# RMS-norm factors of a two-layer decoder trunk: from logarithm, exponential and a Newton step to GpSimd's power operation

## The chip, the core and the metric

One core of one Trainium2 chip runs the whole kernel. The metric is the device time of one execution in microseconds (us), as a median of several runs. The core's engines are PE (TensorE: matmuls, with the weight loads PEld), DVE (VectorE), ACT (ScalarE), POOL (GpSimd) and SP (SyncE, which here only issues DMAs). Each engine works through its own queue in order.

## The reference, cut to what matters

Two layers act on 512 tokens of width 1024 in float32. Layer 0 mixes with an mLSTM (4 heads), layer 1 with stick-breaking attention (16 heads); each layer then cross-attends into 256 memory tokens and applies a SwiGLU FFN of width 2816. Every sub-layer is normalised before and after:

```python
def rms_norm(x, gain):
    y = x * lax.rsqrt(jnp.mean(x * x, axis=-1, keepdims=True) + RMS_EPS)
    return y * gain
...
for layer in range(2):
    y = mixer(rms_norm(x, g[0]));                        x = x + rms_norm(y, g[1])
    y = memory_cross_attention(rms_norm(x, g[2]), mem_n); x = x + rms_norm(y, g[3])
    y = swiglu_ffn(rms_norm(x, g[4]));                   x = x + rms_norm(y, g[5])
```

The memory tokens are normalised once (`mem_n`), and the mLSTM normalises each head's output over its 256 columns. So each norm needs one factor per token, the reciprocal root of a mean square plus 1e-6; with 128 tokens on the partitions that is a 128x1 tile (128x4 for the four mLSTM heads).

## The kernel before

**Work.** All weights stream from HBM. Most products run in float32r on a high and a low part of each operand (`split`, L525: ACT or DVE copies the high part, DVE subtracts for the low part), three matmuls per product (`mm3`). Large projections use a seven-product block scheme (`seven`, L638), in which some weight blocks are summed by accumulating DMAs on POOL's queue (`gather`, L415): such a DMA waits until DVE and ACT have read the old block, and PE needs its sum.

**Order.** The program does not fix the order by hand. `Plan.op` (L148) records each operation with a cost in ns; `Plan.lay_out` (L195) then plays list scheduling over PE, ACT, DVE, POOL and SP, with costs, hand-over latencies (L138) and a limited number of buffers (L36 to L42: 44 big ones, 8 PSUM banks), and the instructions are emitted in the order of the planned starts. An operation on POOL is planned at 110 ns plus 3.4 ns per element (L446), a DMA issue on POOL at 1040 ns (L412). ACT's functions live in tables: Exp and Ln share one, Tanh, Sigmoid and Silu have others (L357); a change of table is planned at 1300 ns (L137), and the load of the Exp/Ln table is emitted at L339. Since the whole order comes out of the planned costs, any change of an operation moves others too.

**Norms.** `sumsq` (L733) squares a tile on ACT and accumulates the sum per token. `rstd` (L738) makes the factor: DVE scales the sum (L743), ACT takes the logarithm (L745) and the exponential of minus one half of it (L746), and DVE does a Newton step in two instructions (L748 and L751), three for the 128x4 tile. Where a row of 1024 is summed in two halves, `rest` (L754) turns the first half's sum into two biases by two DVE instructions. Factors are used in four places:

- `arrive` (L1546): 4 tiles of the input x, at the start; the first tile in halves.
- `heads` (L985): 4 factors of 128x4, for the mLSTM heads. The four PSUM banks of a token tile stay occupied until DVE has multiplied them by the factor (L1005). In the same stage the gates use Sigmoid.
- `boundary` (L816): after each mixer, cross-attention and FFN, 4 token tiles. Each tile has a factor for the post-norm (L841), whose product DVE adds to the residual (L846), and, but for the last boundary, a factor for the next pre-norm (L856), after which the tile is scaled (L859) and PE transposes it (L860). That is 24 and 20 factors. POOL also issues the loads of the gains (L763) and the spills of x (L855).
- `memory` (L1293): 2 tiles, by `rsqrt` (L719), a root by bit shift and three Newton steps, all on DVE.

At the last boundary `out` is stored by SP (L847) after L846.

Of the kernel before, what the change touches and what calls it, by code (L numbers as in the profile page):

```python
# [11 lines left out]
I32 = mybir.dt.int32  # L12
# [4 lines left out]
P = 128  # L17
# [355 lines left out]
class Trunk:  # L373
# [79 lines left out]
    def ts(self, out, a, s1, s2, op0, op1=None):  # L453
        def fn(nc):
            kw = {} if op1 is None else {"op1": op1}
            nc.vector.tensor_scalar(out=ap(out), in0=ap(a), scalar1=ap(s1), scalar2=ap(s2), op0=op0, **kw)  # L456

        self._dve(out, [a], fn, fast=True, scalars=(s1, s2))
# [260 lines left out]
    def rsqrt(self, y, v, n=1):  # L719

        vh, bits, u = self.small(n), self.small(n, I32), self.small(n)
        self.ts(vh, v, -0.5, None, ALU.mult)
        self.ts(bits, v.bitcast(I32), 1, None, ALU.logical_shift_right)
        self.ts(y.bitcast(I32), bits, -1.0, float(0x5F3759DF), ALU.mult, ALU.add)
        for _ in range(3):
            if n == 1:
                self.ts(u, y, y, vh, ALU.mult, ALU.mult)
            else:
                self.tt(u, y, y, ALU.mult)
                self.tt(u, u, vh, ALU.mult)  # L730
            self.stt(y, u, 1.5, y, ALU.add, ALU.mult)

    def sumsq(self, src, acc):  # L733

        junk = self.half(src.free, dt=BF16)
        self.act(junk, src, AF.Square, accum=acc)

    def rstd(self, ss, size, part=None):  # L738

        n = ss.free  # L740
        y, vh, u = self.small(n), self.small(n), self.small(n)
        b, bh = part if part else (self.eps, -0.5 * EPS)
        self.ts(vh, ss, -0.5 / size, bh, ALU.mult, ALU.add)  # L743
        self.act(y, ss, AF.Ln, scale=1.0 / size, bias=b)
        self.act(y, y, AF.Exp, scale=-0.5)  # L745
        if n == 1:  # L746
            self.ts(u, y, y, vh, ALU.mult, ALU.mult)
        else:  # L748
            self.tt(u, y, y, ALU.mult)
            self.tt(u, u, vh, ALU.mult)  # L750
        self.stt(y, u, 1.5, y, ALU.add, ALU.mult)  # L751
# [891 lines left out]
```

## Time and profile before

| | |
|---|---|
| time, median of 3 runs | 1495.97 us (1494.13 to 1496.73) |
| the profiled execution's own time | 1499.86 us |
| its span, first to last instruction | 1498.2 us |
| mean granted TensorE clock | 0.996 of 2.4 GHz |
| instructions | 26046 |
| bytes moved by DMA | 190.46 MB, 127 GB/s over the span |

The profiled execution is one run of its own; its time stands 3.9 us above the median. In the rows, an engine's busy time is the time in which an instruction of its own runs; "idle before" is what the engine waited, and the name behind the arrow is what ended that wait by the trace (for several awaited things, the one that came last). Line numbers are those of helpers where a helper records every operation: L505 is a matmul, L519 a transpose, L451 a two-input DVE operation, L456 DVE's tensor by scalars, L463 DVE's three-operand form, L429 an ACT function, L436 an ACT copy, L413 a DMA issue and L418 an accumulating DMA. Names are kinds of buffers: big, half, sm (the small tiles of the norms), ps (PSUM).

### The profile page before, as it was taken

The page shows a single profiled execution, that of the slowest core. Times are in us where ns is not written, and L with a number is a line of the kernel's source. Part 1 is how long each engine was busy: PE and PEld are TensorE (multiplying, and loading weights), DVE is VectorE, ACT ScalarE, POOL GpSimd, SP SyncE. Part 2 cuts the span into 40 slices and gives each one's busy share as a digit, 9 for nine tenths or more (in the row PEclk, how much of TensorE's full clock was granted, in tenths as well). Part 3 has the DMA queues.
Part 4 walks back from the last instruction along what each step waited for, and adds up shares of the span by engine and source line. Part 5 has one row for each costly group of instructions (what it writes and reads, how often), then busy time and mean ns, then how long its engine had stood idle before and what let it go on. Part 6 is the DMA issues. An engine that isn't in the chain of part 4 may idle for free. (4 is left out here: it accounts for less than half of the span.)

```text
span 1498.2 us, 26046 instructions
## 1 busy us (share of the span) xinstructions
PE 1470.4 (98%) x10346; PEld 1372.4 (92%) x10346; DVE 1214.7 (81%) x1920; ACT 863.6 (58%) x1533; POOL 142.6 (10%) x179
## 2 busy tenths in 40 slices
PE   6999899999999999999999999999999999999998
PEld 5999889998999999998889889888988999999996
DVE  7978879797887876888858998879787969768985
ACT  6668746474754454635548897756456635444632
POOL 2100100100111110110100000000000111110110
PEclk9999999999999999999999999999999999999999
DMA  7545747342654665565511215336514573854651
GB/s 240 113 85 115 223 129 237 71 128 85 203 107 100 132 150 129 118 145 187 166 32 29 71 45 182 113 119 175 143 57 140 116 167 58 205 119 86 141 170 56
DMA packets 166810, 190.46 MB, mean 127 GB/s; under 512 B 6944, under 2 KB 140576, under 8 KB 166688
## 3 DMA queue, kind: packets, MB, share of 16 engines
q1 hardware_dynamic: 119632, 121.16, 25.4%
q0 software_dynamic: 47056, 67.64, 23.0%
q8 instruction: 81, 1.33, 0.4%
q14 instruction: 41, 0.34, 0.1%
HBM read 176.72 MB, written 10.49 MB: 125 GB/s over the span
## 5 line engine op out<-in xcount | busy, mean ns | idle before, releaser
L505 PE MATMUL ps<-big,big 128*128 128x256 f32 (+2 forms) x9712 | 1407.3, 305 | 7.0 <-ACT big L436 3.5
L505 PEld LDWEIGHTS ps<-big,big 128*128 128x128 f32 x9712 | 1294.1, 189 | 93.5 <-ACT big L436 3.9
L451 DVE TENSOR_TENSOR big<-big,big 128x1024 fp32r<-128x1024 f32 (+1 forms) x516 | 607.2, 1210 | 48.9 <-ACT big L436 30.0
L436 ACT CAST big<-big 128x1024 fp32r<-128x1024 f32 (+1 forms) x385 | 391.2, 1044 | 139.9 <-DMA big<-in_ffn_w_gate_up_dram 42.1
L429 ACT ACTIVATE half<-ps 128x512 f32<-128x512 f32 (+4 forms) x185 | 92.5, 527 | 108.0 <-PE ps L505 99.7
L436 ACT COPY half<-ps 128x512 f32<-128x512 f32 (+2 forms) x105 | 61.4, 585 | 137.6 <-PE ps L505 124.9
L451 DVE TENSOR_TENSOR big<-ps,big 128x512 fp32r<-128x512 f32 (+3 forms) x188 | 109.6, 603 | 32.5 <-ACT big L436 20.3
L436 ACT CAST big<-ps 128x512 fp32r<-128x512 f32 (+2 forms) x164 | 80.2, 516 | 91.8 <-PE ps L505 55.2
L451 DVE TENSOR_TENSOR big<-half,big 128x512 fp32r<-128x512 f32 (+3 forms) x150 | 82.7, 575 | 9.3 <-ACT big L429 7.6
L429 ACT ACTIVATE half<-big 128x512 bf16<-128x512 f32 (+1 forms) x63 | 41.9, 665 | 73.1 <-DVE big L451 47.0
L418 POOL DMA_DIRECT2D big<-in_ffn_w_gate_up_dram x40 | 50.8, 1271 | 330.6 <-DVE big L451 171.1
L463 DVE SCALAR_TENSOR_TENSOR half<-ps,half 128x512 f32<-128x512 f32 (+3 forms) x74 | 47.2, 644 | 42.0 <-ACT half L436 22.3
L436 ACT CAST big<-half 128x512 fp32r<-128x512 f32 (+3 forms) x109 | 51.9, 529 | 23.1 <-DVE half L451 14.6
L519 PE MATMUL ps<-const,big 128*128 128x128 f32 (+1 forms) x314 | 44.2, 280 | 13.0 <-DVE big L463 9.9
L451 DVE TENSOR_TENSOR half<-ps,half 128x512 f32<-128x512 f32 (+2 forms) x78 | 46.9, 630 | 11.7 <-PE ps L505 8.1
L519 PEld LDWEIGHTS ps<-const,big 128*128 128x128 f32 (+1 forms) x314 | 37.9, 146 | 18.7 <-issue 10.3
L429 ACT ACTIVATE half<-half 128x512 f32<-128x512 f32 (+2 forms) x74 | 40.4, 588 | 21.1 <-DVE half L451 21.0
L451 DVE TENSOR_TENSOR big<-ps,gain 128x512 f32<-128x512 f32 x32 | 22.0, 686 | 33.4 <-ACT half L429 32.9
L429 ACT ACTIVATE big<-ps 64x512 fp32r<-64x512 f32 (+2 forms) x66 | 38.9, 590 | 11.9 <-PE ps L505 8.1
L505 PE MATMUL ps<-big,const 128*128 128x256 f32 (+3 forms) x224 | 40.5, 320 | 0.0
L505 PEld LDWEIGHTS ps<-big,const 128*128 128x128 f32 x224 | 35.6, 188 | 3.7
L463 DVE SCALAR_TENSOR_TENSOR big<-big,sm,gain 128x512 f32<-128x512 f32 (+1 forms) x47 | 36.3, 805 | 2.6 <-DMA gain<-in_norm_gains_dram 2.0
(85 smaller groups left out, 590.2 us busy)
## 6 DMA issues: line engine op xcount, KB each, us to landing
big<-in_ffn_w_gate_up_dram SPq DMA_DIRECT2D x68, 512.0 KB, 5.7
big<-in_ffn_w_gate_up_dram POOLq DMA_DIRECT2D x40, 512.0 KB, 6.0
big<-in_ffn_w_down_dram SPq DMA_DIRECT2D x36, 512.0 KB, 5.8
big<-in_xa_w_kv_dram SPq DMA_DIRECT2D x32, 512.0 KB, 5.3
big<-in_sb_w_qkv_dram SPq DMA_DIRECT2D x24, 512.0 KB, 3.9
big<-in_ml_w_in_dram SPq DMA_DIRECT2D x19, 512.0 KB, 5.5
dr<-big POOLq DMA_DIRECT2D x16, 512.0 KB, 4.9
big<-in_xa_w_o_dram SPq DMA_DIRECT2D x16, 512.0 KB, 6.2
```

What stands on the lines that cost most here:

```text
L418: "POOL", 1040, lambda nc: nc.gpsimd.dma_start(ap(out), ap(in_), accum_op=ALU.add), [in_, out], [out], load=ns
L429: nc.scalar.activation(ap(out), ap(in_), func, scale=ap(scale), **kw)
L436: "ACT", 0.833 * n + (60 if psum else 95), lambda nc: nc.scalar.copy(ap(out), ap(in_)), [in_], [out],
L451: self._dve(out, [a, b], lambda nc: getattr(nc, q).tensor_tensor(out=ap(out), in0=ap(a), in1=ap(b), op=op), eng)
L463: lambda nc: nc.vector.scalar_tensor_tensor(out=ap(out), in0=ap(a), scalar=ap(s), in1=ap(b), op0=op0, op1=op1),
L505: nc.tensor.matmul(ap(out), lhsT=ap(a), rhs=ap(b), start=start, stop=stop, **kw)
L519: nc.tensor.transpose(ap(out), ap(in_), ap(ident))
```

## The change

`sumsq` scales its input by one over the root of the size before it squares, so that the accumulated sum is the mean square. `rstd` becomes two POOL instructions: add epsilon (or the first half's prepared mean square), then raise to the power of a constant tile of -0.5. `rest` becomes one POOL addition. `rsqrt` goes, and the memory tokens use `rstd` too. The planner, its costs and all hand-written orders stay as they are; the schedule is laid out anew from the changed operations.

```diff
-    def ts(self, out, a, s1, s2, op0, op1=None):
+    def ts(self, out, a, s1, s2, op0, op1=None, eng="DVE"):
...
-    def sumsq(self, src, acc):
+    def sumsq(self, src, acc, size):
...
-        self.act(junk, src, AF.Square, accum=acc)
+        self.act(junk, src, AF.Square, scale=size**-0.5, accum=acc)
...
-    def rstd(self, ss, size, part=None):
-        n = ss.free
-        y, vh, u = self.small(n), self.small(n), self.small(n)
-        b, bh = part if part else (self.eps, -0.5 * EPS)
-        self.ts(vh, ss, -0.5 / size, bh, ALU.mult, ALU.add)
-        self.act(y, ss, AF.Ln, scale=1.0 / size, bias=b)
-        self.act(y, y, AF.Exp, scale=-0.5)
-        if n == 1:
-            self.ts(u, y, y, vh, ALU.mult, ALU.mult)
-        else:
-            self.tt(u, y, y, ALU.mult)
-            self.tt(u, u, vh, ALU.mult)
-        self.stt(y, u, 1.5, y, ALU.add, ALU.mult)
+    def rstd(self, ms, rest=None):
+        y = self.small(ms.free)
+        if rest is None:
+            self.ts(y, ms, EPS, None, ALU.add, eng="POOL")
+        else:
+            self.tt(y, ms, rest, ALU.add, "POOL")
+        self.tt(y, y, self.mhalf[:, 0 : ms.free], ALU.pow, "POOL")
         return y
-    def rest(self, ss):
-        b = self.small(2)
-        for i, m in ((0, 1.0), (1, -0.5)):
-            self.ts(b[:, i : i + 1], ss, m / D, m * EPS, ALU.mult, ALU.add)
-        return b[:, 0:1], b[:, 1:2]
+    def rest(self, ms):
+        b = self.small(1)
+        self.ts(b, ms, EPS, None, ALU.add, eng="POOL")
+        return b
...
-        self.eps = self.const(P, 1)
-        self.memset(self.eps, EPS)
+        self.mhalf = self.const(P, 4)
+        self.memset(self.mhalf, -0.5)
...
-            self.prenorm(m, m, g, steps=True)
+            self.prenorm(m, m, g)
```

The calls in `arrive`, `heads` and `boundary` change with these signatures alone.

## Rows read from the trace of the kernel before

**Rows 1.** The page, busy time, share of the span and instructions of each engine

```profile
PE 1470.4 (98%) x10346; PEld 1372.4 (92%) x10346; DVE 1214.7 (81%) x1920; ACT 863.6 (58%) x1533; POOL 142.6 (10%) x179
```

**Rows 2.** Stretches: length, busy us of PE, PEld, DVE, ACT, POOL; clock, DMA, GB/s

```profile
0.00:30.00 30.00, 18.40 (x77) 15.10 (x78) 19.85 (x39) 20.13 (x40) 9.59 (x37) 1.00 0.77 263
...
125.00:200.00 75.00, 70.02 (x498) 66.01 (x497) 60.37 (x174) 48.74 (x108) 9.94 (x15) 0.95 0.56 164
...
670.00:700.00 30.00, 27.39 (x206) 25.80 (x206) 25.06 (x30) 14.51 (x18) 1.87 (x4) 1.00 0.70 229
...
1485.00:1498.20 13.20, 5.83 (x26) 4.35 (x24) 6.53 (x14) 2.44 (x8) 0.00 (x0) 0.81 0.21 79
```

**Rows 3.** Timeline, head stage: start us, us, instruction, idle before

```profile
134.08 0.16 DVE L456 TENSOR_SCALAR sm<-sm 128x4 f32<-128x4 f32 x1
134.48 1.28 ACT L339 ACT_TABLE_LOAD   x1
...
136.36 1.27 POOL L418 DMA_DIRECT2D big<-in_ml_w_in_dram  x1 [18.07 <-DVE big L451]
...
140.73 0.46 DVE L463 SCALAR_TENSOR_TENSOR big<-ps,sm,big 128x256 f32<-128x256 f32 x1
...
141.24 5.01 PE L505 MATMUL ps<-big,big 128*128 128x256 f32 x40 [1.15 <-DVE big L463]
```

**Rows 4.** Timeline, the late gather after the head stage

```profile
153.90 1.28 POOL L418 DMA_DIRECT2D big<-in_ml_w_in_dram  x1 [1.29 <-DVE sm L456]
...
163.84 1.04 ACT L436 CAST big<-big 128x1024 fp32r<-128x1024 f32 x1 [3.27 <-DMA big<-in_ml_w_in_dram]
```

**Rows 5.** Busy time after the late gather, columns as in group 2

```profile
164.00:174.00 10.00, 8.18 (x44) 7.99 (x45) 6.77 (x14) 6.84 (x15) 0.53 (x1) 0.66 1.04 410
```

**Rows 6.** Waits of PE over the span: total us, times, longest us

```profile
PE ps L519 <- DVE big L451: 1.4, 1, 1.4
```

**Rows 7.** Timeline, the tail of the kernel

```profile
1492.12 0.19 ACT L429 ACTIVATION_READ_ACCUMULATOR half<-big 128x1 f32 x1
...
1492.47 0.68 DVE L451 TENSOR_TENSOR big<-big,gain 128x512 f32<-128x512 f32 x1
...
1493.57 1.41 DVE L463 SCALAR_TENSOR_TENSOR big<-big,sm,big 128x512 f32<-128x512 f32 x2
```

**Rows 8.** Waits of PE weight loads from 1100 to 1180 us

```profile
PEld ps L519 <- DVE big L463: 0.4, 1, 0.4
```

**Rows 9.** Groups of ACT instructions by shape: busy us, mean ns, idle before

```profile
L429 ACT ACTIVATE sm<-sm,sm 128x1 f32<-128x1 f32 x45 | 13.1, 294 | 2.0 <-DVE sm L456 0.7
...
L429 ACT ACT_TABLE_LOAD x8 | 10.3, 1283 | 0.1
L339 ACT ACT_TABLE_LOAD x8 | 10.3, 1283 | 0.1
L429 ACT ACTIVATE sm<-sm 128x1 f32<-128x1 f32 x48 | 9.7, 204 | 1.3
```

**Rows 10.** Groups of DVE instructions by shape

```profile
L451 DVE TENSOR_TENSOR big<-big,big 128x1024 fp32r<-128x1024 f32 x419 | 500.5, 1218 | 41.6 <-ACT big L436 29.3 <-PE ps L505 9.3 <-issue 1.6
...
L456 DVE TENSOR_SCALAR sm<-sm,sm 128x1 f32<-128x1 f32 x99 | 23.7, 242 | 16.5 <-ACT half L429 8.8 <-ACT sm L429 6.1
...
L456 DVE TENSOR_SCALAR sm<-sm 128x1 f32<-128x1 f32 x130 | 15.2, 147 | 11.7 <-ACT half L429 9.4
```

**Rows 11.** Groups of POOL instructions by shape

```profile
L487 POOL TENSOR_SCALAR_AFFINE_SELECT half<-half 128x128 f32<-128x128 f32 x2 | 0.6, 305 | 0.0
...
L482 POOL MEMSET const<- 128x1 f32 x1 | 0.1, 100 | 0.3 <-POOLq L1630 0.3
```

**Rows 12.** Timeline, the first 10 us

```profile
5.20 1.83 POOL L487 TENSOR_SCALAR_AFFINE_SELECT half<-half 128x512 f32<-128x512 f32 x3
...
6.10 0.94 DVE L463 SCALAR_TENSOR_TENSOR sm<-sm,sm 128x1 f32<-128x1 f32 x1
...
9.03 0.75 DVE L463 SCALAR_TENSOR_TENSOR big<-big,sm,gain 128x512 f32<-128x512 f32 x1 [1.98 <-DMA gain<-in_norm_gains_dram]
```

More of the change, by code (lines that the diff above doesn't have):

```diff
@@ L451, in tt @@
         self._dve(out, [a, b], lambda nc: getattr(nc, q).tensor_tensor(out=ap(out), in0=ap(a), in1=ap(b), op=op), eng)
-    def ts(self, out, a, s1, s2, op0, op1=None):
+    def ts(self, out, a, s1, s2, op0, op1=None, eng="DVE"):
+        q = {"DVE": "vector", "POOL": "gpsimd"}[eng]
         def fn(nc):
             kw = {} if op1 is None else {"op1": op1}
-            nc.vector.tensor_scalar(out=ap(out), in0=ap(a), scalar1=ap(s1), scalar2=ap(s2), op0=op0, **kw)
-        self._dve(out, [a], fn, fast=True, scalars=(s1, s2))
+            getattr(nc, q).tensor_scalar(out=ap(out), in0=ap(a), scalar1=ap(s1), scalar2=ap(s2), op0=op0, **kw)
+        self._dve(out, [a], fn, eng, fast=True, scalars=(s1, s2))
     def stt(self, out, a, s, b, op0, op1):
@@ L763, in gain, with prenorm @@
         return g
-    def prenorm(self, out, x, g, steps=False):
+    def prenorm(self, out, x, g):
         ss = self.small(1)
-        self.sumsq(x, ss)
-        if steps:
-            v, r = self.small(1), self.small(1)
-            self.ts(v, ss, 1.0 / D, EPS, ALU.mult, ALU.add)
-            self.rsqrt(r, v)
-        else:
-            r = self.rstd(ss, D)
-        self.stt(out, x, r, g, ALU.mult, ALU.mult)
+        self.sumsq(x, ss, D)
+        self.stt(out, x, self.rstd(ss), g, ALU.mult, ALU.mult)
     def acts(self, n=S):
@@ L835, in evac @@
             x = ps if not ys else y
-            self.sumsq(x, s)
+            self.sumsq(x, s, D)
             self.tt(y, x, g_post[:, sl], ALU.mult)
@@ L840, in evac @@
                 return
-            r = self.rstd(s, D, part[t])
+            r = self.rstd(s, part[t])
             x, y, ss2 = xs[t], yg[t], self.small(2)
@@ L848, in evac @@
                 else:
-                    self.sumsq(x[:, c], ss2[:, hf : hf + 1])
+                    self.sumsq(x[:, c], ss2[:, hf : hf + 1], D)
                     if hf == 0:
@@ L855, in evac @@
                 self.dma("POOL", spill[t], x)
-            r = self.rstd(ss2[:, 1:2], D, part[t])
+            r = self.rstd(ss2[:, 1:2], part[t])
             for hf in range(2):
@@ L994, in heads @@
                 self.tt(dh, ps[:, 256:257], dh, ALU.max)
-                self.sumsq(ps[:, 0:256], ss[:, hh : hh + 1])
+                self.sumsq(ps[:, 0:256], ss[:, hh : hh + 1], MLV)
                 nums.append(ps)
@@ L1000, in heads @@
             self.tt(vv, vv, rinv, ALU.mult)
-            y = self.rstd(vv, MLV)
+            y = self.rstd(vv)
             self.tt(y, y, rinv, ALU.mult)
@@ L1553, in arrive @@
         for i, c in enumerate(halves):
-            k.sumsq(xin[t][:, c], ss[:, i : i + 1])
-        r = k.rstd(ss[:, 1:2], D, k.rest(ss[:, 0:1]))
+            k.sumsq(xin[t][:, c], ss[:, i : i + 1], D)
+        r = k.rstd(ss[:, 1:2], k.rest(ss[:, 0:1]))
         for i, c in enumerate(halves):
```

11 lines of the change are left out of this document (removed).

## The prediction

> **What bounds the kernel.** I read the page first: PE is busy 1470.4 us of 1498.2, DVE 81%, ACT 58%, POOL 10% [rows 1]. PE's matmuls are the same before and after, so only PE's idle time and PE at a low clock can change: 27.8 us are idle in all. The second view cuts the span into stretches [rows 2]: 11.6 us of the idle time lie in the first 30 us, 5.0 between 125 and 200 us, 2.6 between 670 and 700, and 7.4 at the end; the other 1.2 us are strewn. The reader should see that DVE and ACT, which the change relieves, are not where the time is: what they save counts only where PE waits for them.
>
> Such a place is the mLSTM head stage. In its timeline [rows 3] the scaled squares of the first head tile are ready at 134.24 (134.08 + 0.16), but ACT must load the Ln/Exp table, goes back to Sigmoid, loads again, and the tile's first product starts at 140.73, 6.5 us later. The product frees a PSUM bank, and PE, idle for 1.15 us, starts at 141.24, 0.05 us after its end at 141.19. Then follows a stall whose owner is a transfer: an accumulating DMA is issued on POOL at 153.90, and ACT's copy of its block starts at 163.84 after waiting 3.27 us for it [rows 4]. With the 1.15 us and a wait of 1.41 us for DVE at 181 [rows 6] taken from the stretch's 4.98, this stall is 2.42 us. It also costs clock: in the 10 us after 164 the granted clock is 0.66 in the mean, thus at the lower level of 1.2 GHz for some 7 us, and 44 matmuls take 8.18 busy us [rows 5], where 40 took 5.01 at 141 [rows 3]. At that rate 44 take 5.5 us, so the clock costs 2.7 us. The stall was PE's idle time just before.
>
> The tail is read as a chain [rows 7]: the last accumulation ends at 1492.31 (1492.12 + 0.19), the last scaled products start at 1493.57: 1.26 us from sum to factor. Last I looked for norms that PE only just escapes: before the second FFN one transpose's weight load waited 0.4 us for DVE's scaled tile [rows 8].
>
> **The change, part by part.** *Off ACT.* 52 factors lose Ln and Exp, 0.294 and 0.204 us each by the rows for most of them [rows 9]: about 26 us. There are 17 table loads: the first, eight to Ln/Exp and eight to others, at 1.283 us [rows 9]. In the timeline I count which serve a norm alone: four in the head stage with the four that lead back, and the one before the last boundary; two more only move on to the next Exp. Nine go, 11.5 us. *Off DVE.* The first scaling and the Newton step (93 of the 99 instructions with two small operands, 22.5 us) and the two of `rest` for 45 sums with seven like them (97 of 130, 11.3 us) [rows 10], with some 12 us in smaller groups: 46 us of 1214.7. All this is hidden behind PE, except in the places above, so by itself it is worth nothing.
>
> *Onto POOL.* 54 factors of two instructions and 45 of `rest` make 153, on an engine that is busy 142.6 us [rows 1]. No arithmetic of one element stands in the trace on POOL. The nearest below is a memset of 128x1, 0.10 us; the nearest that reads SBUF is a select of 128x128, 0.305 us [rows 11]; the longest POOL instruction in these rows is a DMA issue, 1.27 us [rows 3]. I take 0.305 for the addition and for the power, 0.10 as the lower end of both, and 1.27 as the upper end of the power alone. Three hand-overs (ACT to POOL, POOL to itself, POOL to DVE) I take at the 0.05 us seen from DVE to PE. From sum to factor that is 0.15 + 0.61 = 0.76 us, between 0.35 and 1.73, against 1.26 now. At the tail this gives -0.5 us (-0.9 to +0.5). DVE's product with the gain, at 1492.47 [rows 7], now waits behind the scaling that goes; it will run before, so POOL finds DVE idle there.
>
> *The head stage.* The factor needs about 0.8 us and one small DVE product. POOL's queue is in order, and an accumulating DMA stands in it, waiting, until 136.36, and takes until 137.63 [rows 3]. Even behind that the factor is there by about 138.6, 2 us ahead of 140.73. So the 1.15 us go. But PE then comes to the late block 1.15 us sooner, so that stall shrinks only by as much as the block comes sooner. What hangs on norms there is ACT's and DVE's work in front of the DMA's issue: the ACT loads and functions named above are half of ACT's time from 134 to 154. What does not is the DMA itself: 9.9 us from issue to use, with the DMA engines at a share of 1.04 [rows 4, 5]. Of the 2.42 + 2.7 = 5.1 us I take one half, 2.6; the ends are 0 and 5.1. The wait at 181 stands in a stretch in which DVE works without a break, partly on the two memory factors by bit shift, 20 small instructions; I take 0.3 of its 1.41.
>
> *The start.* The first factor is ready at 7.04 and waits for the gain's DMA until 9.03 [rows 12]. With POOL busy on selects until 7.03 it may come 0.76 us after them, at 7.8: still covered. I take 0. If that cover went, 0.8 us would show.
>
> *Waits added.* A norm that waits at the head of POOL's queue holds back what is behind it: accumulating DMAs, gain loads, spills, and so weights for PE. In the FFNs, where most accumulating DMAs are, no norm runs; at the boundaries PE has matmuls to cover it. I take 0, and leave a loss to the second rival.
>
> Sum: -1.15 - 2.6 - 0.3 - 0.5 = -4.55 us. On the profiled execution's 1499.86 that gives 1495.3; the median of the runs is 3.9 us lower, so I forecast 1495.97 - 4.55 = **1491.4 us**. Its own range is 1487 to 1493: all of 5.1 and 0.9 at one end, a gain of 3 at the other. About 0.2%, 3.0 us, is what a measurement of this kernel can tell from no change.
>
> **The rivals.** *The stall moves.* If the late block is as late in absolute time as before, PE waits 1.15 us longer for it, and the whole head stage gives nothing; the sum is then -0.5 - 0.3, and the time 1495.2 (1493 to 1499, since the whole order is laid out anew and other waits of 1 to 3 us, such as the 2.6 us before 700, can come or go). For it speaks the DMA share of 1.04, against it that the DMA's issue itself waits on DVE and ACT.
>
> *POOL and DVE block each other.* In the first 10 us a DVE instruction on three 128x1 operands took 0.94 us, against a mean of 0.24 for others as small; it ended at 7.04, just as three POOL selects ended at 7.03 [rows 10, 12]. So a small DVE instruction was held until POOL was done, and the reverse must be feared: DVE's commonest instruction takes 1.218 us and stands there 419 times [rows 10]. If each POOL instruction waits half of one, 0.61 us, a factor takes 0.76 + 1.22 = 1.98 us, 0.72 more than now. Of the 40 factors of the five boundaries that are followed by transposes I take one in four as uncovered, since one weight load of a transpose already waits [rows 8]: 10 x 0.72 = 7.2 us, and 1503.2 us. It decides from the point where the factor takes longer than 1.26 plus what PE still has to do. Against it: PE idles nowhere at these boundaries now, and the factor's present way also waits for DVE's long instructions. The Trainium skill, page "SBUF — State Buffer", section "Who interferes with whom", states this as a rule: a DVE instruction with two SBUF inputs and a GpSimd one that reads SBUF exclude each other, and the later one waits for the whole of the first. By that rule this change is slower, and the 0.94 us agree with it; no row shows the reverse case, POOL held by DVE. A slow power alone, at its upper 1.27 us, works in the same place: 0.15 + 0.305 + 1.27 = 1.73 us are 0.47 more than now, 4.7 us on 10 factors.
>
> **How the numbers follow.** Forecast 0.50, moved stall 0.27, blocked POOL 0.23. So faster by over 0.2% 0.50, within 0.27, slower 0.23. The range runs from 1487 (the forecast with its best ends) to 1501, which takes in the moved stall and the milder part of the blocked POOL, and leaves out under 2 in 10.
>
> **What would show it.** Right: eight table loads; no Sigmoid load between two head tiles; no PE wait for DVE's product near 141; the late block's copy before 163 and a granted clock above 0.66 behind it; POOL powers near 0.3 us; sum to factor under 1.26 us at the tail. Wrong: powers over 1 us, POOL's norms starting as long DVE instructions end, waits of transposes on DVE's scaled tile at the boundaries, or accumulating DMAs issued later than now because a norm stands in front of them.

## The result, and the profile after

The changed kernel takes **1503.53 us** (median; 1501.89 to 1506.04), against 1495.74 us for the kernel before on the same chip: a ratio of 1.0053, 95% interval 1.0041 to 1.0065, so 7.8 us slower. The forecast was 1491.4 us, faster, with a range of 1487 to 1501. Of all executions below, one of the kernel with raised boundary prices and multiplications fell in a slower state (1788.08 us, granted clock 0.754 in the mean); ratios leave it out.

The page after, busy time, share of the span and instructions of each engine; then the stretches of [rows 2], with the same columns, and the 10 us of [rows 5]:

```profile
span 1501.8 us, 25849 instructions
...
PE 1471.7 (98%) x10346; PEld 1371.4 (91%) x10346; DVE 1178.0 (78%) x1649; ACT 830.1 (55%) x1421; POOL 219.0 (15%) x332
```

```profile
0.00:30.00 30.00, 19.09 (x87) 15.79 (x88) 18.16 (x23) 19.55 (x35) 15.77 (x47) 1.00 0.80 266
125.00:200.00 75.00, 71.49 (x507) 66.44 (x506) 58.21 (x139) 41.46 (x101) 23.54 (x34) 0.98 0.65 196
670.00:700.00 30.00, 30.00 (x216) 28.00 (x216) 27.03 (x32) 14.68 (x18) 1.45 (x3) 1.00 0.68 227
...
164.00:174.00 10.00, 9.20 (x79) 8.96 (x78) 9.24 (x17) 8.56 (x16) 2.42 (x3) 1.00 0.96 371
```

Against [rows 1], ACT is relieved by 33.5 us (37.5 reckoned) and DVE by 36.7 (46 reckoned), and POOL is 76.4 us busier. In the first two stretches PE idles 0.7 and 1.5 us less than in [rows 2], and behind the late block the clock is 1.00, against 0.66 [rows 5]. So up to there the head stage, which the forecast watched, is better. The 2.6 us of the third stretch are gone too, but a second profile of the kernel before lacks them as well. What is new is the list of transposes that wait for the tile they transpose. At the boundaries the kernel before has none of 0.15 us or more. This is the timeline of PE after, the seven of them:

```profile
236.50 0.66 PE L521 MATMUL ps<-const,big 128*128 128x128 f32 x4 [0.79 <-DVE big L465]
...
383.62 1.23 PE L521 MATMUL ps<-const,big 128*128 128x128 f32 x8 [0.75 <-DVE big L465]
...
707.81 0.63 PE L521 MATMUL ps<-const,big 128*128 128x128 f32 x4 [0.45 <-DVE big L465]
...
717.00 0.66 PE L521 MATMUL ps<-const,big 128*128 128x128 f32 x4 [0.47 <-DVE big L465]
...
731.58 0.63 PE L521 MATMUL ps<-const,big 128*128 128x128 f32 x4 [0.28 <-DVE big L465]
...
1014.48 0.66 PE L521 MATMUL ps<-const,big 128*128 128x128 f32 x4 [1.08 <-DVE big L465]
...
1150.65 1.23 PE L521 MATMUL ps<-const,big 128*128 128x128 f32 x8 [0.48 <-DVE big L465]
```

Together 4.3 us, spread over all five boundaries. In front of each stands a factor made on POOL. The groups of POOL (out<-in, shape, count, busy us, mean ns) give what one costs: the power, the additions of eps, and the additions of a prepared rest.

```profile
L451 POOL TENSOR_TENSOR sm<-sm,const 128x1 f32<-128x1 f32 x50 | 31.6, 632 | 3.4
L458 POOL TENSOR_SCALAR sm<-sm 128x1 f32<-128x1 f32 x50 | 21.0, 421 | 242.6 <-ACT half L429 241.2
...
L451 POOL TENSOR_TENSOR sm<-sm,sm 128x1 f32<-128x1 f32 x45 | 12.4, 276 | 105.7 <-ACT half L429 104.6
```

A power takes 0.57 us in the median (0.55 at least), an addition 0.19 to 0.22 where nothing holds it (spans on POOL are rough, but a product of DVE that waits for a free power also starts 0.60 us after the power did, 194.21 after 193.61). The means are larger because some are held. The timeline of the tile in front of the first wait shows how, with POOL's and DVE's rows and ACT's last sum:

```profile
233.43 1.31 POOL L458 TENSOR_SCALAR sm<-sm 128x1 f32<-128x1 f32 x1 [2.27 <-ACT half L429]
234.82 0.19 POOL L451 TENSOR_TENSOR sm<-sm,sm 128x1 f32<-128x1 f32 x1
235.09 0.57 POOL L451 TENSOR_TENSOR sm<-sm,const 128x1 f32<-128x1 f32 x1
...
233.44 1.22 DVE L451 TENSOR_TENSOR big<-big,big 128x1024 fp32r<-128x1024 f32 x1
235.69 1.41 DVE L465 SCALAR_TENSOR_TENSOR big<-big,sm,gain 128x512 f32<-128x512 f32 x2 [1.03 <-POOL sm L451]
...
233.82 0.19 ACT L429 ACTIVATION_READ_ACCUMULATOR half<-big 128x1 f32 x1
```

The rest of the first half, 0.22 us when free, starts at 233.43 and lasts 1.31: it ends at 234.74, 0.08 us after DVE's instruction that began at 233.44. The sum of the second half is there at 234.01; its addition has to wait 0.81 us behind that rest. From sum to product the factor takes 1.68 us, and the transpose comes 0.79 us late. This is the case that no row of before showed, POOL held by DVE. By the Trainium skill, page "SBUF — State Buffer", section "Who interferes with whom", the later of two such instructions waits for the whole of the first; the 1.31 us agree with it, although the two starts, 0.01 us apart, do not tell which came first.

Not every long instruction of DVE holds POOL. These are POOL and DVE on another tile, whose gain product reads one operand from PSUM:

```profile
193.34 0.19 POOL L451 TENSOR_TENSOR sm<-sm,sm 128x1 f32<-128x1 f32 x1 [3.12 <-ACT half L429]
193.61 0.57 POOL L451 TENSOR_TENSOR sm<-sm,const 128x1 f32<-128x1 f32 x1
...
193.22 0.69 DVE L451 TENSOR_TENSOR big<-ps,gain 128x512 f32<-128x512 f32 x1 [4.13 <-ACT half L429]
```

The addition lies wholly inside DVE's product and takes 0.19 us. In this trace 33 of POOL's additions, rests and powers on 128x1 take over 0.1 us more than a free one; each of them overlaps a DVE instruction with two SBUF operands, and none of those that overlap only products with a PSUM operand is held.

The second way in which a factor comes late is POOL's own queue. The last tile of the second cross-attention's boundary, rows of POOL, DVE and ACT:

```profile
1157.16 1.38 POOL L418 DMA_DIRECT2D big<-in_ffn_w_gate_up_dram  x1 [6.57 <-ACT half L429]
1158.06 0.71 POOL L451 TENSOR_TENSOR sm<-sm,sm 128x1 f32<-128x1 f32 x1
1158.71 0.61 POOL L413 DMA_DIRECT2D gain<-in_norm_gains_dram  x1
1159.34 0.59 POOL L451 TENSOR_TENSOR sm<-sm,const 128x1 f32<-128x1 f32 x1
...
1157.51 1.21 DVE L451 TENSOR_TENSOR big<-big,big 128x1024 fp32r<-128x1024 f32 x1
1159.97 1.42 DVE L465 SCALAR_TENSOR_TENSOR big<-big,sm,big 128x512 f32<-128x512 f32 x2 [1.25 <-POOL sm L451]
...
1156.67 0.19 ACT L429 ACTIVATION_READ_ACCUMULATOR half<-ps 128x1 f32 x1
```

The sum is ready at 1156.86, the product starts at 1159.97, 3.11 us later (2.4 in the kernel before at this tile): a weight's accumulating DMA is issued in front of the addition, and a gain's load between addition and power, and the addition is held until DVE's product of 1157.51 ends. PE does not wait for this one in the profile: the tile's transposes start at 1164.42 with no wait of 0.15 us before them. In front of the longest of the seven waits (1014.48) the queue does count. POOL's rows on that tile, for its post-norm factor:

```profile
1007.57 0.19 POOL L451 TENSOR_TENSOR sm<-sm,sm 128x1 f32<-128x1 f32 x1 [6.31 <-ACT half L429]
1008.93 0.64 POOL L413 DMA_DIRECT2D gain<-in_norm_gains_dram  x1 [1.17 <-DVE big L451]
1009.59 0.58 POOL L451 TENSOR_TENSOR sm<-sm,const 128x1 f32<-128x1 f32 x1
```

The power starts 1.83 us after the addition's end, since the gain's load between them waits for DVE to have read the old gain. From sum to product this takes 2.78 us (2.40 before at this tile). The tile of the first wait has the same pattern, with 2.91 us (2.56 before).

### The profile page after: what moved, and what is told of

It is laid out like the page before. It is cut to its first block, busy times and chain, and to the rows that moved or that the text cites. A ratio compares the mean times of both kernels' runs of the same rounds, so it can differ in the third digit from the quotient of the medians.

```text
span 1501.8 us, 25849 instructions
## 1 busy us (share of the span) xinstructions
PE 1471.7 (98%) x10346; PEld 1371.4 (91%) x10346; DVE 1178.0 (78%) x1649; ACT 830.1 (55%) x1421; POOL 219.0 (15%) x332
## 4 chain that ended last, share of the span: by engine, by line
PE 47%; DVE 1%; ACT 1%; POOL 1%; DMA 1%; issue 1%; POOLq 0%; DVEq 0%; ACTq 0%
PE ps L507 46%; PE ps L521 1%; DVE big L451 1%; DMA big<-in_ffn_w_down_dram 1%; DVE big L465 0%; POOL sm L451 0%; ACT half L429 0%; ACT big L436 0%; DVE half L451 0%; POOL sm L458 0%; ACT big L429 0%; DVE half L458 0%; POOL dr L413 0%; DVE half L437 0%; DVEq L1615 0%
## 5 line engine op out<-in xcount | busy, mean ns | idle before, releaser
L507 PE MATMUL ps<-big,big 128*128 128x256 f32 (+1 forms) x9712 | 1405.4, 305 | 4.8 <-ACT big L436 2.5
L451 DVE TENSOR_TENSOR big<-big,big 128x1024 fp32r<-128x1024 f32 (+1 forms) x516 | 607.8, 1213 | 42.6 <-ACT big L436 23.2
L451 DVE TENSOR_TENSOR big<-ps,big 128x512 fp32r<-128x512 f32 (+3 forms) x188 | 109.1, 604 | 35.4 <-ACT big L436 20.2
L451 DVE TENSOR_TENSOR big<-half,big 128x512 fp32r<-128x512 f32 (+3 forms) x150 | 82.8, 578 | 8.1 <-ACT big L429 7.3
L458 POOL TENSOR_SCALAR sm<-sm 128x1 f32<-128x1 f32 (+1 forms) x54 | 25.3, 469 | 264.4 <-ACT half L429 241.2
L436 ACT CAST big<-half 128x512 fp32r<-128x512 f32 (+4 forms) x110 | 51.5, 523 | 17.6 <-DVE half L451 12.6
L451 DVE TENSOR_TENSOR big<-ps,gain 128x512 f32<-128x512 f32 x32 | 22.1, 690 | 44.5 <-ACT half L429 44.1
L451 DVE TENSOR_TENSOR half<-ps,half 128x512 f32<-128x512 f32 (+2 forms) x78 | 46.9, 632 | 10.3 <-PE ps L507 5.7
L465 DVE SCALAR_TENSOR_TENSOR big<-big,sm,big 128x512 f32<-128x512 f32 x48 | 33.9, 749 | 12.1 <-POOL sm L451 12.1
```

The source lines that it names most:

```text
L436: "ACT", 0.833 * n + (60 if psum else 95), lambda nc: nc.scalar.copy(ap(out), ap(in_)), [in_], [out],
L451: self._dve(out, [a, b], lambda nc: getattr(nc, q).tensor_tensor(out=ap(out), in0=ap(a), in1=ap(b), op=op), eng)
L458: getattr(nc, q).tensor_scalar(out=ap(out), in0=ap(a), scalar1=ap(s1), scalar2=ap(s2), op0=op0, **kw)
L465: lambda nc: nc.vector.scalar_tensor_tensor(out=ap(out), in0=ap(a), scalar=ap(s), in1=ap(b), op0=op0, op1=op1),
L507: nc.tensor.matmul(ap(out), lhsT=ap(a), rhs=ap(b), start=start, stop=stop, **kw)
```

## The experiments

Four theories were set against each other, and the expectations use their letters. **A**: at the boundaries the factor's way over POOL is too long for where its transposes stand. **B**: the loss is luck, since every change lays the whole order out anew. **C**: the way is not too long, the planner has the wrong price for it; it plans an operation of one element on POOL at 113 ns (L446 before), the power too, so that with its hand-overs a factor is planned at 0.77 us. **D**: the way over POOL is too slow or blocked in itself; it loses wherever it stands, whatever the plan. Each ratio below is to the kernel before on the same chip, with its 95% interval. "Waits at boundaries" counts PE's waits of more than 0.15 us in front of a transpose, behind 190 us, in the profiled execution.

| kernel | us | ratio | waits at boundaries |
|---|---|---|---|
| changed kernel | 1503.53 | 1.0053 (1.0041 to 1.0065) | 7, 4.3 us |
| powers in the heads only | 1493.59 | 0.9989 (0.998 to 0.9997) | none |
| powers at the boundaries only | 1504.46 | 1.006 (1.0046 to 1.0074) | 6, 3.5 us |
| boundary powers as multiplications | 1495.59 | 1.0008 (0.9996 to 1.0019) | 2, 0.7 us |
| powers planned at 570 ns | 1502.77 | 1.0052 (1.0038 to 1.0065) | 3, 0.7 us |
| all prices raised | 1500.12 | 1.0032 (1.0022 to 1.0043) | 1, 0.25 us |
| before, factors underpriced | 1512.16 | 1.0108 (1.0094 to 1.0122) | 5, 1.8 us |
| changed kernel, laid out anew | 1500.80 | 1.0042 (1.0027 to 1.0057) | 7, 4.3 us |
| additions on DVE | 1510.49 | 1.0094 (1.008 to 1.0108) | 16, 10.7 us |
| gains loaded by SP | 1501.55 | 1.0044 (1.0028 to 1.0059) | 6, 3.9 us |
| logarithms at the boundaries | 1491.77 | 0.9974 (0.9962 to 0.9985) | none |
| boundary prices raised | 1497.53 | 1.001 (1.0001 to 1.0019) | 1, 0.2 us |
| the same, powers as multiplications | 1496.37 | 1.0002 (0.9993 to 1.0012) | 1, 0.2 us |
| boundary prices at bare durations | 1498.88 | 1.0026 (1.0015 to 1.0036) | 3, 1.4 us |
| logarithms, laid out anew | 1491.40 | 0.9969 (0.9958 to 0.998) | none |
| before, laid out anew | 1496.08 | 1.0 (0.9991 to 1.001) | none |

**The kernel before once more**, unchanged.

> The kernel before, unchanged, in another profiled execution. The first profiled execution took 1499.86 us, 4 us above its median, and had a late weight block at 163 us (2.4 us of PE idle and some 2.7 us of work at the lower clock). If that stall belongs to the execution and not to the kernel: span about 1494, no PE idle of over 1 us between 160 and 170, no drop of the granted clock there; then there was nothing for the change to win. If it belongs to the kernel: span about 1498 and the stall again.

1496.47 us, span 1494.8: the span as in the first of the two cases, the stall as in the second. The late block's stall is there again (PE waits 2.04 and 0.71 us at 165 and 166). The 2.6 us idle before 700 of [rows 2] are not: a stray stall that comes and goes, and much of why the first profiled execution stood 3.9 us above the median.

**One half of the change at a time.** The kernel before, with the new factor in the head stage alone:

```diff
-            y = self.rstd(vv, MLV)
+            y = self.rstd_pow(vv)
```

> The kernel before with only the four mLSTM head factors by POOL's power; boundaries, input and memory by logarithm and exponential. Theory A: no loss, 1493 to 1496 (a gain of up to 3 from the head stage, where table loads go). Theory B: anything between 1493 and 1503, since the order is laid out anew here as well.

and with the new factor and rest at the boundaries alone:

```diff
-            r = self.rstd(s, D, part[t])
+            r = self.rstd_pow(s, part[t])
...
-            r = self.rstd(ss2[:, 1:2], D, part[t])
+            r = self.rstd_pow(ss2[:, 1:2], part[t])
```

> The kernel before with only the boundaries' 44 factors and their partial sums by POOL; heads, input and memory by logarithm and exponential. Theory A: the whole loss is here, 1502 to 1505, with transposes waiting for DVE's scaled tile at the boundaries. Theory B: anything between 1494 and 1505, and waits that are not at the boundaries.

1493.59 us, faster than both kernels, and 1504.46 us, slower than both. So the sign is not that of POOL as such (D falls, in so far as it says wherever): four factors over POOL gain, 44 lose.

**A cheaper operation in the power's place**, the order on every engine being the same. The boundary factors are then not computed, so other values run through the kernel:

```diff
-        self.tt(y, y, self.mhalf[:, 0 : ms.free], ALU.pow, "POOL")
+        self.tt(y, y, self.mhalf[:, 0 : ms.free], ALU.mult if fake else ALU.pow, "POOL")
...
-            r = self.rstd(s, part[t])
+            r = self.rstd(s, part[t], True)
...
-            r = self.rstd(ss2[:, 1:2], part[t])
+            r = self.rstd(ss2[:, 1:2], part[t], True)
```

> The changed kernel with the same instructions in the same order on every engine; only the 44 powers of the boundaries are multiplications by the same constant, so the boundary factors are not computed (the heads, the input and the memory keep the power). Theory A (the factor's way through POOL is too long at the boundaries and PE's transposes wait for it): the POOL instruction falls from 0.57 to about 0.2 us, the transposes' waits shrink, time 1498 to 1500. Theory B (the new layout of the whole order is at fault, with stalls elsewhere): 1503 as the changed kernel.

1495.59 us: by the medians 7.9 us come back without one instruction having moved, by the ratios 6.7 (the executions scatter from 1493.92 to 1503.79). That excludes luck as the whole cause; in this order the loss hangs on the power's duration. Where it is lost the profiles show only in part: the two profiled spans are 4.4 us apart (1501.8 and 1497.4), of which the waits at the boundaries are 3.6.

**What the planner believes.** The changed kernel with the power planned at 570 ns, and with all new POOL instructions planned at their measured time with hand-overs:

```diff
-            ns = 110 + n * 3.4
+            ns = cost or 110 + n * 3.4
...
+        self._dve(out, [a, b], lambda nc: getattr(nc, q).tensor_tensor(out=ap(out), in0=ap(a), in1=ap(b), op=op), eng, cost=570 if op == ALU.pow else None)
```

> The changed kernel, but the planner is told 570 ns for a power on POOL (what the trace shows) in place of 113. Same instructions, other order. Theory C (the loss is a wrong price: PE's transposes are planned 0.4 us too early behind every factor): the boundaries' waits go, 1492 to 1496. Theory D (POOL's way is too slow or blocked in itself, by DVE and by DMA issues on its queue, whatever the plan): still 1501 to 1505.

```diff
+        cost = {ALU.pow: 640 if out.free == 1 else 1050}.get(op, 360)
...
+        self._dve(out, [a], fn, eng, fast=True, scalars=(s1, s2), cost=430 if out.free == 1 else 1050)
```

> As planned_pow, but the planner is told the means with blocking: 360 and 430 ns for the additions, 640 for the power (1050 for the 128x4 ones). Theory C: 1492 to 1496, a bit above planned_pow if the plan is now too cautious, below it if blocking by DVE matters. Theory D: 1501 to 1505.

1502.77 and 1500.12 us, where C had 1492 to 1496 for both; the first lies in the range that D had. The waits of transposes nearly go, but the time does not follow: the whole order moves, the head stage with it. With the power at 570 ns PE waits 3.01 us at 1017 for DVE's part of a matmul behind the fourth boundary's last transposes, and 1.14 at 287. With all prices raised the late block's stall is back (PE waits 2.46 and 0.87 us at 165 and 166), and PE waits 0.95 us at 290. These two runs change two things at once and settle nothing; the priced runs further down were made for that.

**The mirror**: the kernel before, told that a factor takes 0.76 us.

```diff
-        n = ss.free
+        n, first = ss.free, len(self.plan.ops)
...
+        if n == 1:
+            for o in self.plan.ops[first:]:
+                o.ns = 20
+                o.alts = {o.eng: (20, o.fn)}
```

> The mirror: the kernel before, same instructions, but the planner is told 20 ns for each of the instructions of a 128x1 factor, so that a factor is planned at 0.76 us from its sum, as in the changed kernel, where the trace shows 1.1 to 1.5. Nothing runs on POOL. Theory C: slower by 4 to 10 us, 1500 to 1506, with transposes waiting at the boundaries. Theory D: 1494 to 1498.

1512.16 us, 16 us lost by a price alone, more than the 1500 to 1506 that C had. Not all at the boundaries (1.8 us of waits there): PE also waits 3.56 and 0.68 us at 59 and 64, and 2.00 at 1444.

**The changed kernel with another assumed delay to PE**, 130 ns for 120 (L139 before), which lays the order out anew.

> The changed kernel with the planner's latency into PE at 130 ns in place of 120, a change of the layout that means nothing (272 of 19738 lines of PE's order differ). It tells how much a new layout alone moves: theories C and D both 1502 to 1505; if it comes out below 1499 or above 1507, the loss was the luck of one layout.

1500.80 us, with the seven waits in the same places (4.3 us). So a new order alone is worth 2.7 us here. The two profiled spans are 4.0 us apart (1501.8 and 1497.8): 1.4 us is one stall in the last FFN, for a down weight (2.55 us in the changed kernel, 1.18 here), and 2.4 us are lost in the changed kernel before 185 us, as is told further down; the loss at the boundaries stays.

**Less on POOL**: all additions go back to DVE.

```diff
-            self.ts(y, ms, EPS, None, ALU.add, eng="POOL")
+        self.ts(y, ms, EPS if rest is None else rest, None, ALU.add)
```

> The changed kernel, with the 50 additions of eps or of the rest, and the rests themselves, done by DVE; only the 50 powers stay on POOL, one instruction per norm in place of two or three. It separates two parts of theory A (the boundaries lose because the way over POOL is longer than the order allows). A1, the power's own 0.57 us, planned at 0.11, is what is late: the power is still there and a hand-over goes from ACT to DVE to POOL to DVE, so the time stays at 1501 to 1505, with waits of transposes at the boundaries as in the changed kernel (4 us in all). A2, it is POOL's queue and DVE's hold on POOL (additions of 0.22 us that took 0.7 to 1.7, rests behind a spill's issue): with 100 fewer POOL instructions most of the 8 us comes back, 1496 to 1499, and the factor of the last tiles falls from about 3 us to 2 or below. Theory B (luck of the order): anything from 1494 to 1504.

1510.49 us, 7 us worse than the changed kernel, outside all that was expected. Two rows of DVE on one tile tell why (ACT's sum there is ready at 1011.97):

```profile
1012.01 0.69 DVE L451 TENSOR_TENSOR big<-ps,gain 128x512 f32<-128x512 f32 x1 [0.96 <-ACT half L429]
1012.61 0.21 DVE L458 TENSOR_SCALAR sm<-sm,sm 128x1 f32<-128x1 f32 x1
```

DVE's gain product (L451) waits for ACT's square, as the sum does, and stands ahead of the addition; so the addition starts 0.64 us after the sum, where POOL's own ran beside that product. From sum to product most tiles now take 1.5 us instead of 1.03, with the power still planned at 113 ns, and the waits grow to 16 (10.7 us). A longer factor costs more, which is A from the other side; but by the planner's costs the factor is at 0.71 us here (129 and 113 ns, and hand-overs of 140, 130 and 200), so it is also later against its plan, as C would have it. On such tiles POOL's second instruction was not the harm, since it ran beside DVE.

**Gains loaded by SP** in place of POOL.

```diff
-        self.dma("POOL", g, row.broadcast_to([P, D]))
+        self.dma("SP", g, row.broadcast_to([P, D]))
```

> The changed kernel, with the loads of the gains issued by SP in place of POOL, so that no gain load stands between a norm's addition and its power on POOL's queue (as at the last tile of the second cross-attention boundary, 0.61 us of 3.11). If A2 holds (POOL's queue), the last tiles' factors fall from 3.1 to about 2.4 us and the time by 1 to 2 us, to 1501.5 to 1502.5. If A1 holds (the power's own time), the time stays within 1 us of 1503.5. Theory B: the order is laid out anew, 1499 to 1506, with no change at the last tiles.

1501.55 us, as one part of POOL's queue would have it. At the last tiles of the two cross-attentions the factors fall less than was asked, from 3.11 to 2.60 and 2.95 us, but at those of the two mixers from 2.91 and 2.78 to 1.78, and PE's waits behind them from 0.79 and 1.08 to 0.44 and 0.56. Other waits come in their place (0.92 at 393, 1.17 at 1162), and 2 us are no more than the new order gave above, so the share of the queue stays open. Moving the spills off POOL's queue as well was not tried.

**Logarithms back at the boundaries**, everything else as changed.

```diff
-            r = self.rstd(s, part[t])
+            r = self.rstd_log(s, part[t])
...
-            r = self.rstd(ss2[:, 1:2], part[t])
+            r = self.rstd_log(ss2[:, 1:2], part[t])
```

> The changed kernel with the 44 factors of the five boundaries and of the end taken back to logarithm, exponential and Newton step; the powers stay for the first rows, the memory rows and the heads. Theory A: as the kernel with powers in the head stage alone (1493.6), less up to 0.8 us, since the first rows arrived 0.8 us earlier in the changed kernel (30.1 against 30.9 us): 1492.5 to 1494, ratio 0.998 to 0.999, and no transposes that wait at the boundaries. Theory B (luck of the order): 1490 to 1500. Theory D (every factor over POOL costs time, wherever it stands): above 1494, since 6 more factors than in that kernel go over POOL.

1491.77 us, 4.1 us below the kernel before and the best of the computation so far. Its page, and its head stage and the 10 us behind the late block:

```profile
PE 1466.4 (98%) x10346; PEld 1368.8 (92%) x10346; DVE 1207.7 (81%) x1867; ACT 852.0 (57%) x1512; POOL 160.3 (11%) x200
```

```profile
125.00:200.00 75.00, 71.76 (x513) 66.74 (x512) 58.92 (x150) 42.74 (x105) 21.30 (x27) 1.00 0.62 190
...
164.00:174.00 10.00, 8.98 (x76) 8.50 (x74) 9.27 (x17) 9.17 (x18) 2.43 (x3) 1.00 0.88 342
```

**Prices raised at the boundaries alone**, so that the first 185 us keep their order.

```diff
-            ns = 110 + n * 3.4
+            ns = getattr(self, "price", None) or 110 + n * 3.4
...
-                part[t] = self.rest(s)
+                part[t] = self.rest(s, 430)
...
-            r = self.rstd(s, part[t])
+            r = self.rstd(s, part[t], 360, 640)
...
-            r = self.rstd(ss2[:, 1:2], part[t])
+            r = self.rstd(ss2[:, 1:2], part[t], 360, 640)
```

> The changed kernel, computing the same; only the planner's prices of the boundaries' 44 factors and of their rests are raised to what they take with their hand-overs in the trace (addition 360 ns, power 640, rest 430; the planner's own are 113). The head stage, the memory rows and the first rows keep the planner's own prices, so that the first 185 us stay as in the changed kernel; in the earlier run with the prices raised everywhere the head stage was laid out anew and its stall of 2.5 us came back. Theory C (the loss is the planner's: it lets transposes come before the factor is ready): no transposes that wait at the boundaries (4.3 us of waits in the changed kernel's profile), the gain of the head stage stays, and the time is 1492 to 1496. Theory A (the way over POOL is itself too long, whatever the plan): with the plan knowing it, the boundaries still lose about 1 us each, 1499 to 1503. Theory B: 1494 to 1504.

1497.53 us: 6.0 of the 7.8 us come back. POOL's instructions are held as before, but PE now has other matmuls in front of the transposes. Rows of POOL on the same tile as above:

```profile
231.91 0.61 POOL L451 TENSOR_TENSOR sm<-sm,sm 128x1 f32<-128x1 f32 x1 [0.49 <-ACT half L429]
232.60 1.44 POOL L451 TENSOR_TENSOR sm<-sm,const 128x1 f32<-128x1 f32 x1
```

The power takes 1.44 us here, and no transpose waits for it. Theory C had asked for 1496 at most, so it holds for the larger part, not for all. Not all of the 6.0 us need lie at the boundaries, though. Rows of PE on the same instructions, in the changed kernel and here:

```profile
176.38 0.44 PE L521 MATMUL ps<-const,big 128*128 128x128 f32 x2 [1.88 <-DVE big L451]
...
184.97 1.04 PE L521 MATMUL ps<-const,big 128*128 128x128 f32 x8
```

```profile
175.62 0.44 PE L521 MATMUL ps<-const,big 128*128 128x128 f32 x2 [1.39 <-DVE big L451]
...
182.61 1.03 PE L521 MATMUL ps<-const,big 128*128 128x128 f32 x8
```

The order is the same up to there, yet this execution is 2.4 us ahead. In the changed kernel's the granted clock falls behind the wait of 1.88 us (0.73 from 175 to 180, 0.93 from 180 to 185), here it stays at 1.00. From this transpose to the end of the span the changed kernel takes 1316.8 us, this one 1311.2: 5.6 us less.

**The same order, the boundary powers as multiplications.**

```diff
-        self.tt(y, y, self.mhalf[:, 0 : ms.free], ALU.pow, "POOL")
+        self.tt(y, y, self.mhalf[:, 0 : ms.free], ALU.mult if add else ALU.pow, "POOL")
```

> The kernel with the boundaries' prices raised (1497.5), in the same order on every engine, with the 44 boundary powers made multiplications with the same operands (the boundaries' factors then have another value; the outputs of the norms are another computation). It asks what the power's own time still costs once the plan makes room for it. If the rest of the loss (5.8 us against 1491.8 of the kernel with logarithms at the boundaries) is the power's 0.57 us on the path: 1493 to 1495.5. If it is the order or the queue (additions, rests and powers behind transfers on POOL, a query weight that comes 3 us later at 256 to 274): 1496.5 to 1498.

1496.37 us, between the two expectations and nearer to the second: 1.2 us for the power's own time, which is not clear of zero, as the two intervals overlap (0.9993 to 1.0012, and 1.0001 to 1.0019). In the changed kernel the same edit was worth 7.9 us by the medians, 6.7 by the ratios. So a power that is planned for costs a small part of one that is not.

**Bare durations as prices.**

```diff
-                part[t] = self.rest(s, 430)
+                part[t] = self.rest(s, 223)
...
-            r = self.rstd(s, part[t], 360, 640)
+            r = self.rstd(s, part[t], 190, 570)
```

> As the kernel with the boundaries' prices raised, with the bare durations in their place (addition 190 ns, power 570, rest 223; hand-overs are the planner's own 200 ns), so a factor is planned at about 1.3 us against 1.6 there and 0.77 in the changed kernel, and measures 1.0 to 1.1 where nothing holds it. Theory C (price): also without waits of transposes for late factors, or with a few (under 1.5 us), 1495 to 1499. Theory A: 1499 to 1503. If the order's luck is worth more than the price (theory B): outside of 1495 to 1499 without a sign of its own.

1498.88 us with 1.4 us of waits, as C had it: the recovery comes from the price, and most of it is there with the bare durations. This profile is the cleaner comparison with the changed kernel's, since the first 185 us are as slow in both (the same wait of 1.88 us, the same transpose at 185.22): from there to the end it takes 1312.3 us against 1316.8, so 4.5 us come back behind 185.

**What an order alone is worth at both ends**: the kernel with logarithms at the boundaries and the kernel before, each with 130 ns for 120.

```diff
-    TO_PE = 120
+    TO_PE = 130
```

> The kernel with logarithms at the boundaries and powers elsewhere (1491.8), with the planner's assumed delay to PE at 130 ns in place of 120: the same computation in a slightly other order. If that kernel's lead over the changed one is a matter of where the factors are made (theory A with C): within 3 us of 1491.8, and below the kernel before still, 1490 to 1494.5. If its time was a lucky order (theory B): 1495 or above.

> The kernel before, with the same 130 ns in place of 120. It shows what a new order alone is worth at the other end. If an order alone is worth up to 3 us (as from 1503.5 to 1500.8 in the changed kernel): 1493 to 1499, so that only the part of the 7.8 us above some 3 us speaks of the change. If it is worth more, 1500 or above, the change's loss could be an order's luck (theory B).

1491.40 and 1496.08 us, 0.4 and 0.3 us from their originals. So the 4 us between the two ends do not look like an order's luck, as far as one other order of each can tell.

## Why the prediction was wrong, point by point

**What held.** *The relief of ACT and DVE* has nearly its size (33.5 and 36.7 us of 37.5 and 46) and, by itself, no value: 8 table loads in place of 17, as counted. *The head stage* does what was said. Timeline after, POOL, DVE and ACT, to set beside [rows 3, 4]:

```profile
132.79 0.33 POOL L458 TENSOR_SCALAR sm<-sm 128x4 f32<-128x4 f32 x1 [15.70 <-DVE sm L451]
133.21 1.05 POOL L451 TENSOR_TENSOR sm<-sm,const 128x4 f32<-128x4 f32 x1
134.49 0.48 DVE L465 SCALAR_TENSOR_TENSOR big<-ps,sm,big 128x256 f32<-128x256 f32 x1
...
149.28 1.31 POOL L418 DMA_DIRECT2D big<-in_ml_w_in_dram  x1 [0.52 <-ACT big L436]
...
159.55 1.05 ACT L436 CAST big<-big 128x1024 fp32r<-128x1024 f32 x1 [1.92 <-DMA big<-in_ml_w_in_dram]
```

The first product starts at 134.49 (140.73 before), the late block's DMA is issued 4.6 us sooner and its copy starts 4.3 us sooner, the wait of 1.15 us is gone (waits of 0.37 at 142.34 and 0.45 at 154.43 are there), and so is the stall of 2.42 us. PE waits 0.80 at 166.99, but not for the late block: for ACT's copy of a PSUM tile, which stands behind the square of a memory tile that came late by DMA. Behind the block the clock is granted in full until 175 us. So the rival "the stall moves" falls: the issue did wait for DVE and ACT. The factor's price was not right even here, since a power of four columns takes 1.05 us and not 0.305; but the accumulating DMA that the forecast had in front of it comes behind it, at 136.40, so the factor is early all the same.

**What was mis-sized.** The head stage was put at -3.75 us; alone it measures 1.9 us by the medians (1495.5 to 1493.59; 0.4 to 3.0 by the interval), and 3.9 by the spans of two profiled executions (1494.8 to 1490.9). The 1.41 us at 181, of which 0.3 were to go, have become 1.88 at 176.4, and behind them stands the low clock shown above, for which the forecast had no term: from 176.38 to 184.97 PE does in 8.6 us what takes 7.0 where the clock stays at 1.00 (175.62 to 182.61). It is not in every execution with this order of the first 185 us; with logarithms at the boundaries (wait 1.65) it is absent. The start was costed at nothing; PE's second transpose starts at 12.02 in place of 12.68 and 12.22, and the first rows are all transposed by 30.08, against 31.36 and 30.91 in the two profiles of before. That this is the power's is not shown: with powers in the heads alone, where the start is as before, they are transposed by 30.30. The kernel with logarithms at the boundaries holds all of the gain that the forecast had but for the tail: 4.05 us forecast, 4.1 measured. That the sums agree is partly chance, as one term was too large and the rest of the gain has no shown place. The range's lower end was also mis-added: all of 5.1 and 0.9 us give 1488.5, not 1487.

**The step that failed** is "Waits added. [...] at the boundaries PE has matmuls to cover it. I take 0". It argued from before's order, in which PE idles nowhere at the boundaries. But the order is laid out from planned costs, and the planner, told 113 ns for a power of 570, has the transposes stand where it believes the factor ready. The cover that the rows of before showed was the planner's allowance for the old factor, and the change took it away by its price. Where nothing holds it, the new factor is in fact shorter than the old one: 1.03 us against 1.46 from sum to post-norm product (11 of the 24 tiles after), and 1.02 against 1.10 to the pre-norm product, which the transposes await. What counts is not which factor is shorter but which is late against its plan. Before the transposes the old one, at about 1.2 us by the planner's costs, was 0.1 early; the new one, planned at 0.77, is 0.25 late where nothing holds it and 0.9 where DVE does (1.68 above). Where a gain's load stands in POOL's queue, the post-norm factor ahead of it comes after 2.78 to 3.11.

**The tail** was to gain 0.5 us because DVE's gain product "will run before". It does not, for it overwrites the tile that ACT's square still reads, so it starts with the sum, as in [rows 7]. Timeline after, ACT, DVE and POOL:

```profile
1495.35 0.19 ACT L429 ACTIVATION_READ_ACCUMULATOR half<-big 128x1 f32 x1
1495.57 0.69 DVE L451 TENSOR_TENSOR big<-big,gain 128x512 f32<-128x512 f32 x1 [0.79 <-ACT half L429]
1495.62 0.70 POOL L451 TENSOR_TENSOR sm<-sm,sm 128x1 f32<-128x1 f32 x1 [2.88 <-ACT half L429]
1496.39 0.55 POOL L451 TENSOR_TENSOR sm<-sm,const 128x1 f32<-128x1 f32 x1
1496.97 1.41 DVE L465 SCALAR_TENSOR_TENSOR big<-big,sm,big 128x512 f32<-128x512 f32 x2 [0.71 <-POOL sm L451]
```

The addition begins 0.05 us after DVE's product and ends 0.06 us after it: 0.70 us for 0.19. From sum to factor it is 1.43 us against 1.26, a loss of 0.2. In this boundary the gain product reads two SBUF tiles, and all four post-norm factors take 1.43 to 1.46 us.

**The rival that came true** is the second, POOL and DVE blocking each other, with 1503.2 us named for it. Its place (transposes at the five boundaries) is right; its time is right by luck, for it reckoned ten factors of 0.72 us, and the profile has seven waits of 4.3 us in all; its inside is not right. It held each POOL instruction for 0.61 us in the mean; by the groups the hold is about 0.12 us (means above the medians of 570, 223 and 190 ns: 50 x 62, 50 x 198 and 45 x 86 ns make 17 us on 145 instructions), with a few of over 1 us. And it let the loss come from the hold alone, where the power's 0.57 us under a wrong price carries most of it (the slow power that the rival named beside it was put at 1.27 us). The other way round little is lost: DVE's commonest group of two-operand instructions takes 1213 ns in the mean after, 1210 before.

**What stays open.** With the boundaries priced right, the kernel still takes 5.8 us more than with logarithms there. The power's own time is 1.2 of them at most by the medians. PE also waits 0.91 us at 284 for DVE, DVE for ACT's copy, and that for a query weight, whose third accumulating DMA is issued at 274.15, against 270.40 with logarithms. The other 3.7 us are not settled: they may be POOL's queue, or an order that has less room. Stalls in the last FFN for a down weight may be a part: seven of the twelve profiles with boundary factors over POOL or underpriced have one of 1.06 to 2.55 us near 1440; the six of the kernel before, of the heads alone and of the logarithms, each order of them, have none.

## What to carry to other kernels

Where an order is planned from costs, a new operation needs its measured duration in the plan before its time is judged: here the same power cost 7.9 us (6.7 by the ratios) under a price of 0.11 us and 1.2 us, not clear of zero, under a raised one. Slack seen in the trace before is slack of the old plan; it need not be there for an operation whose time the new plan does not know. And an operation should move engines only where its old way was the bound: four factors that cost table loads where PE waited gained by POOL, 44 others whose way was hidden lost, and the mixed kernel (1491.8 us) beats both.

## What the runs showed of the hardware

In the changed kernel's profile POOL takes 0.19 to 0.22 us for an addition on 128x1, about 0.57 us for a power on 128x1 and 1.05 us for one on 128x4. A POOL instruction of one element that meets a DVE instruction with two SBUF operands is held to its end: 0.70 us beside one of 0.69, and 1.31 us beside one of 1.22; beside a product of 0.69 us that reads PSUM an addition took 0.19. Down-weight stalls of about 2 us come and go between executions of one order (1.97 us at 685 in one profile of the kernel before and none in the other; 2.42 us at 1435 with the multiplications under raised prices and none with the powers), and so did a low clock behind 176 us in kernels with the same first 185 us. A single profiled execution stood up to 5.2 us above its median (1501.58 and 1496.37).
